# A hybrid decoder layer on one core: weight splitting of the up-projection and the g2 modulation moved to GpSimd

## The chip, the core and the metric

The kernel runs on one core of a Trainium2 chip. The metric is the device time of one execution in microseconds (us). TensorE multiplies matrices into PSUM banks; VectorE (DVE in the profile), ScalarE (ACT) and GpSimd (POOL) work elementwise, each in the strict order of its own instruction queue; SyncE (SP) issues the transfers from HBM.

## What is computed

One decoder layer on 256 tokens of 1024 channels in float32: an adaptive-norm mixer (recurrent and attention branches) and a gated channel sub-layer. The change lies in the second, and in the modulation vector `g2`, a product of `c` with a part of `w_ada`:

```python
mod = (c @ w_ada[l] + b_ada[l])[:, None, :]
sh1, sc1, g1, sh2, sc2, g2 = jnp.split(mod, N_MOD, axis=-1)
...
h2 = rmsnorm(x, norm2_g[l]) * (1.0 + sc2) + sh2
up = causal_dwconv(h2 @ w_up[l], ffn_conv_w[l], ffn_conv_b[l])
gate, val = jnp.split(up, 2, axis=-1)
x = x + g2 * ((jax.nn.silu(gate) * val) @ w_down[l])
```

## The kernel before

Weights come as a stream of 1 MB chunks [128, 2048] in the order of their use; six raw chunks (tile `w`) are held at a time, and a chunk's buffer is given to the next transfer by `used` and `send` when its last reader has been issued. TensorE multiplies in float32r, so every weight chunk and every activation is split into a high part (`wh`, a cast by ScalarE, `hi`) and a low part (`wl`, raw minus high by VectorE, `lo`); a product is three matmuls: high x high, high x low of the activation, low x high. A chunk is split in two halves of [128, 1024], `part` 0 and 1. Three chunks can be held split (`wspl`).

The channel sub-layer goes through 22 slices of 128 channels. From slice 4 on a plain loop sets the order, and every engine takes its instructions in the order in which the loop writes them. In turn `f`:

- TensorE multiplies `up(f)`: 8 row tiles `kt` of 6 matmuls, 48 in all. Tiles 0 to 3 need half 0 of chunk `up f`, tiles 4 to 7 half 1; within a tile the last two of the six matmuls need `wl`. At the end of the turn it multiplies `down(f - 2)`, 24 matmuls.
- ScalarE and VectorE meanwhile make slice `f - 1` ready: `gated_a` (ACT, from the PSUM bank), `gated_d` (DVE, the convolution), `gated_s` (ACT, Silu), `gated_m` (DVE), `gated_h` (ACT, high part `ph`), `gated_l` (DVE, low part `pl`). Between them they split the chunk of the next slice, `up f + 1`.
- In even turns they first split a chunk of the down-projection, `halves("dn", f // 2 - 1)`, which serves two slices.
- In turns 7, 9, 11 and 13 VectorE also takes a chunk of `g2`: `ada` multiplies each half [128, 1024] by `c` (tile `cb`, the same on all partitions) and sums along the row in the same instruction, and `ada_add` adds the bias. `g2` is used only by `out`, after the last slice.

`Bank.mm` issues all of these matmuls (L65), `affine` all casts of ScalarE (L138). In the profile L166 is `lo`, L367 `ada`, L377 `ada_add`, L732 `gated_a`, L740 `gated_d`, L744 `gated_s`, L748 `gated_m`, L756 `gated_l`.

Of the kernel before, what the change touches and what calls it, by code (L numbers as in the profile page):

```python
# [7 lines left out]
F32 = mybir.dt.float32  # L8
# [15 lines left out]
EPS = 1e-6  # L24
BIG = 1e30
SH1, SC1, G1, SH2, SC2, G2 = range(6)

# columns of the packed per-channel parameters
O_BADA = 0
# [15 lines left out]

# first guesses of an inverse root are these less half the bits, the sign being that before three Newton steps
GUESS = {1: float(0x5f3759df - 0x400000 - (1 << 31)), -1: float(0x5f3759df - 0x400000)}

NW = 6          # raw weight chunks in flight
NSPLIT = 3      # split weight chunks in flight  # L50


class Bank:
    """A PSUM bank that n matmuls accumulate into; the first one opens it, the last one closes it."""

# [13 lines left out]
def hybrid_layer(ctx: ExitStack, tc: tile.TileContext, x_d, c_d, pk_d, bd_d, ada1_d, lin_d, v_d,  # L69
# [20 lines left out]
    def tok(t):  # L90
        """[128, 4, 256] seen as [128, 2, 512]."""
        return flat(t).rearrange("p (t n) -> p t n", t=2)
# [6 lines left out]

# [1 line left out]
    order = []  # L101
# [15 lines left out]
    def send():  # L117
        """The next chunk's transfer."""
        if len(sent) < len(order):
            key = order[len(sent)]  # L120
            sent.append(key)
            raw[key] = wraw.tile([P, 2048], F32, tag="w", name="w")
            uses[key] = {"g1": 1, "ada1": 2, "s2": 2, "g2": 2}.get(key[0], 4)
            n = 1024 if key[0] in ("ada1", "lin") or key in (("g1", 0), ("g1", 1)) else 2048
            for c in range(0, 2048, n):
                nc.sync.dma_start(raw[key][:, c:c + n], srcs[key[0]][key[1]][:, c:c + n])

    def used(key):
        """A chunk's buffer goes to the next one after its last use."""
        uses[key] -= 1  # L130
        if uses[key] == 0:
            send()

    def affine(e, out, in_, scale=None, bias=None):
        """in_ * scale + bias by the activation engine, or by the vector engine where e is 1."""
        if e == 0:
            if scale is None and bias is None:
                nc.scalar.copy(out, in_)  # L138
            elif bias is None:
                nc.scalar.activation(out, in_, AF.Copy, scale=scale)  # L140
            else:
                nc.scalar.activation(out, in_, AF.Identity, scale=1.0 if scale is None else scale, bias=bias)  # L142
        elif scale is None and bias is None:
            nc.vector.tensor_copy(out, in_)
        elif scale is None:
            nc.vector.tensor_scalar(out, in_, bias, None, op0=ALU.add)
        elif bias is None:
            nc.vector.tensor_scalar(out, in_, scale, None, op0=ALU.mult)
        else:
            nc.vector.tensor_scalar(out, in_, scale, bias, op0=ALU.mult, op1=ALU.add)  # L150

    def hi(kind, i, part, e=0):
        """The high part of a half of the chunk, in float32r."""
        key = (kind, i)
# [5 lines left out]

    def lo(kind, i, part):
        """The low part: high + low is exact."""
        key = (kind, i)
        h, l = spl[key]
        c = slice(part * 1024, part * 1024 + 1024)
        nc.vector.tensor_sub(l[:, c], raw[key][:, c], h.bitcast(F32)[:, c])  # L166
        used(key)

# [1 line left out]
    xT = big.tile([P, KT, S], F32, name="xT")  # L170
# [39 lines left out]
    def table(func):  # L210
        """Has the activation engine load a function's table before the data is there."""
        nc.scalar.activation(warm, ones[:, 0:1], func)

    def warm_up(i):
        """Keeps the tensor engine's clock up while the first data comes."""
        b = get(B, "warm", lambda: bank(0, 1))
# [3 lines left out]

    B = {}   # PSUM banks by use
    T = {}   # tiles by use

    def consts():
        # (1 + b) g in b's place, where the gain is (1 + b + w c) g
        for n, j in ((0, SC1), (1, SC2)):
# [13 lines left out]

# [1 line left out]
    def newton(i, m, t, yi, sign):  # L242
        """A step of sign / sqrt(2 m): a first guess from the exponent, then three Newton steps of three."""
        y, v = yi.bitcast(F32), nc.vector
# [12 lines left out]
    def half_mean(ss, count):  # L257
        """-(ss / count + EPS) / 2"""
        m = small.tile([P, 2], F32, tag="hm", name="hm")
# [3 lines left out]
    def inverse(r, m):  # L263
        """1 / r after a Newton step, for r about the root of -2 m."""
        t = small.tile(list(r.shape), F32, tag=f"t{len(r.shape)}", name="t")
# [11 lines left out]
    def spread(d, bk, off):  # L277
        """Per-token values, on the diagonals of d, to all partitions: bank[:, off:off+256]."""
        bk.reopen(2)
# [3 lines left out]
    def token_sums(bk, off, sq):  # L283
        """bank[:, off + 2 th] += sum over the channels of sq [128, 256]."""
        for th in range(2):
# [6 lines left out]

# [1 line left out]
    cb = const.tile([P, D], F32, name="cb")  # L294
# [21 lines left out]
    def norm_s(n):  # L316
        """The roots of the means of the squares of the tokens, a column for each half of them."""
        T["rms"] = small.tile([P, 2], F32, tag="rms", name="rms")
# [12 lines left out]

# [1 line left out]
    lt = const.tile([P, 8, 4], F32, name="lt")  # L333
# [5 lines left out]
    def sp(i):  # L339
        """A step of z (1 + z^2 / 3 + ... + z^18 / 19) 2 + max(-lambda, 0), where z = e / (2 + e) and e = exp(-|lambda|)."""  # L340
        e, d, acc, v = lt[:, 1, :], lt[:, 2, :], lt[:, 3, :], nc.vector
# [18 lines left out]

# [1 line left out]
    def ada(kind, i, a):  # L362
        """Half a chunk: the modulation of 128 channels, by the vector engine; sc with its norm's gain."""
        v = raw[kind, i].rearrange("p (a n) -> p a n", a=2)
# [3 lines left out]
                                       op0=ALU.mult, op1=ALU.add, accum_out=mod[:, j, kt:kt + 1])  # L368
        used((kind, i))

    def ada_add(kind, i):
# [7 lines left out]
    def normed(n, kt):  # L379
        """x times its norm and gain; the shift comes with the split into high and low."""  # L380
        rep = B["n2"].t[:, 256:512] if n else rrep
# [17 lines left out]
    def lin(kt, out, i):  # L399
        """One of the three products of a k-tile for one of the four outputs."""  # L400
        wh, wl = spl["lin", kt]
# [11 lines left out]

# [1 line left out]
    def lru(name):  # L415
# [33 lines left out]
    def root():  # L449
        # sqrt(1 - a^2) = (1 + a) sqrt(tanh(-log(a) / 2))  # L450
        nc.scalar.activation(lru("r"), lru("r"), AF.Sqrt)  # L451
# [60 lines left out]

# [1 line left out]
    def kn():  # L514
# [8 lines left out]
    def q_sum():  # L523
        """The sums over the heads' channels, for two heads on the first rows of each quarter."""
        b = get(B, "qn", lambda: bank(3, 1))
# [31 lines left out]
    def qk_r(i):  # L557
        """The heads' norms, with the other sign."""
        if i < 2:
# [29 lines left out]

# [1 line left out]
    def g1_mm(i, b):  # L591
# [25 lines left out]

# [1 line left out]
    mn = small.tile([P, H, 2], F32, tag="mn", name="mn")  # L619
# [3 lines left out]
    def sc(i):  # L623
        """The scores of two heads, which lie on the two halves of the rows."""
        qs, kT = T["qs"], T["kT"]
# [37 lines left out]

# [1 line left out]
    def o_inv():  # L665
# [28 lines left out]

# [1 line left out]
    def wo(c, kt):  # L696
# [21 lines left out]

# [1 line left out]
    def up(f, kt):  # L720
# [708 lines left out]
    for f in range(4, NF):  # L1429
# [16 lines left out]
        if f + 1 < NF:  # L1446
            lo("up", f + 1, 1)
        if f in (7, 9, 11, 13):
            i = (f - 7) // 2
            ada("g2", i, 0)  # L1450
            ada("g2", i, 1)
            ada_add("g2", i)
        for m in range(KT):
# [24 lines left out]
def _lay_out(i):  # L1478
# [7 lines left out]
    def rows(w, per):  # L1486
        """[K, N] -> [chunks, 128, per * N]: `per` row tiles of 128 in a chunk."""
        k, n = w.shape
        return w.reshape(k // (per * P), per, P, n).transpose(0, 2, 1, 3).reshape(-1, P, per * n)

    def panels(w, n):
        """[1024, N] -> [N / n, 128, 8 * n]: all row tiles of n columns."""
        return w.reshape(KT, P, -1, n).transpose(2, 1, 0, 3).reshape(-1, P, KT * n)
# [52 lines left out]
```

## Time and profile before

| | |
|---|---|
| median of 3 runs | 333.09 us (330.11 to 334.47) |
| span of the profiled execution | 333.0 us |
| busy: TensorE, VectorE, ScalarE, GpSimd | 97%, 80%, 58%, 1% of the span |
| weights and inputs read from HBM | 75.91 MB |
| mean granted TensorE clock | 0.985 of full speed |

The profile gives no other time for the profiled execution than its span, from the first to the last instruction. The busy shares are means over stages with different limits; matmuls are pipelined, so a busy share of TensorE near 100% tells that it never stood still, not that it could not be fed faster.

### The profile page before, as it was taken

To read this page: it belongs to the slowest core of one execution; us is meant where nothing else is said; L and a number is where in the kernel's file an instruction comes from. 1 tells how busy PE (TensorE), PEld (TensorE's weight loads), DVE (VectorE), ACT (ScalarE), POOL (GpSimd) and SP (SyncE) were. 2 spreads that over 40 slices of the span, in tenths; PEclk is the share of its full clock that TensorE was granted. 3 is DMA by queue.
4 is the path that set the end of the run, shared out by engine and by line. 5 is a ranking of instruction groups with operands and counts; after the bars stand their busy time and mean duration, and the time that the engine had idled before them with its cause. 6 is when DMAs were issued, how large, how long until landed. Compare 5 with 4: busy or idle time off the path is not lost.

```text
span 333.0 us, 6442 instructions
## 1 busy us (share of the span) xinstructions
PE 324.4 (97%) x2594; PEld 305.6 (92%) x2594; DVE 266.5 (80%) x523; ACT 192.7 (58%) x329; POOL 2.8 (1%) x15
## 2 busy tenths in 40 slices
PE   7899999999989999999999999999999999999994
PEld 6599999977678999899999999999999999999994
DVE  0689999698999989899685888888888767685654
ACT  4752525499999436877455546464646464555530
POOL 3000000000000000000000000000000000000000
PEclk9769999999999999999999999999999999999999
DMA  6999999907648788972936457584849364300003
GB/s 200 404 407 408 405 336 426 366 5 275 238 160 347 299 323 299 367 280 86 365 134 238 143 204 293 177 330 153 355 139 365 129 226 154 128 0 3 0 2 126
DMA packets 14287, 77.37 MB, mean 232 GB/s; under 512 B 1585, under 2 KB 2225, under 8 KB 7218
## 3 DMA queue, kind: packets, MB, share of 16 engines
q1 hardware_dynamic: 14258, 76.97, 61.4%
q8 instruction: 20, 0.33, 0.4%
q14 instruction: 9, 0.07, 0.1%
HBM read 75.91 MB, written 1.05 MB: 231 GB/s over the span
## 4 chain that ended last, share of the span: by engine, by line
PE 85%; ACT 8%; DVE 3%; DMA 2%; issue 1%; SPq 0%
PE bank L65 85%; ACT p L644 2%; DMA xT<-in_dram 2%; ACT m L434 1%; DVE m L460 1%; ACT pt L138 1%; DVE m L768 1%; ACT wh L138 1%; ACT m L444 1%; ACT m L447 0%; DVE sq L309 0%; ACT L451 0%; ACT L444 0%; ACT L434 0%; DVE m L454 0%
## 5 line engine op out<-in xcount | busy, mean ns | idle before, releaser
L166 DVE TENSOR_TENSOR wl<-w,wh 128x1024 fp32r<-128x1024 f32 x94 | 113.3, 1221 | 19.6 <-ACT wh L138 18.8
L138 ACT CAST wh<-w 128x1024 fp32r<-128x1024 f32 x89 | 90.8, 1042 | 37.9 <-PE bank L65 34.2
L65 PE MATMUL bank<-hh__1580,wh 128*128 128x256 f32 x352 | 71.1, 284 | 0.0
L65 PE MATMUL bank<-hl__1581,wh 128*128 128x256 f32 x352 | 71.0, 283 | 0.0
L65 PE MATMUL bank<-hh__1580,wl 128*128 128x256 f32 x352 | 70.9, 283 | 0.0
L65 PEld LDWEIGHTS bank<-hh__1580,wh 128*128 128x128 f32 x352 | 54.9, 192 | 0.4 <-ACT hh__1580 L142 0.4
L65 PEld LDWEIGHTS bank<-hl__1581,wh 128*128 128x128 f32 x352 | 54.9, 192 | 0.2 <-DVE hl__1581 L394 0.2
L65 PEld LDWEIGHTS bank<-hh__1580,wl 128*128 128x128 f32 x352 | 54.9, 192 | 0.0
L740 DVE SCALAR_TENSOR_TENSOR m<-bank,pk,m 128x255 f32<-128x255 f32 x88 | 40.5, 480 | 17.3 <-ACT m L732 15.7
L65 PE MATMUL bank<-ph,wh 128*128 128x256 f32 x176 | 49.9, 284 | 0.0
L65 PE MATMUL bank<-pl,wh 128*128 128x256 f32 x176 | 49.8, 283 | 0.0
L65 PE MATMUL bank<-ph,wl 128*128 128x256 f32 x176 | 49.8, 283 | 0.0
L732 ACT ACTIVATE m<-bank,pk 128x256 f32<-128x256 f32 x44 | 22.4, 559 | 21.7 <-PE bank L65 21.7
L65 PEld LDWEIGHTS bank<-ph,wh 128*128 128x128 f32 x176 | 33.8, 192 | 0.1
L65 PEld LDWEIGHTS bank<-pl,wh 128*128 128x128 f32 x176 | 33.8, 192 | 0.0
L65 PEld LDWEIGHTS bank<-ph,wl 128*128 128x128 f32 x176 | 33.8, 192 | 0.0
L367 DVE CUSTOM_DVE_ANT_0 w<-w,cb 128x1024 f32<-128x1024 f32 x22 | 26.4, 1219 | 0.0
L744 ACT ACTIVATE m<-m 128x256 f32<-128x256 f32 x22 | 9.2, 418 | 24.9 <-DVE m L740 24.9
L65 PE MATMUL bank<-hh_mix__1172,wh 128*128 128x256 f32 x64 | 18.4, 288 | 0.0
L65 PE MATMUL bank<-hl_mix__1173,wh 128*128 128x256 f32 x64 | 18.2, 284 | 0.0
L65 PE MATMUL bank<-hh_mix__1172,wl 128*128 128x256 f32 x64 | 18.1, 283 | 0.0
L65 PE MATMUL bank<-hh__273,wh 128*128 128x256 f32 x96 | 14.7, 292 | 0.1
(174 smaller groups left out, 444.3 us busy)
## 6 DMA issues: line engine op xcount, KB each, us to landing
w<-in_dram SPq DMA_DIRECT2D x55, 1024.0 KB, 4.9
w<-in_dram SPq DMA_DIRECT2D x32, 512.0 KB, 8.6
xT<-in_dram SPq DMA_DIRECT2D x4, 256.0 KB, 4.8
out_dram<-m SPq DMA_DIRECT2D x4, 128.0 KB, 2.5
out_dram<-m SPq DMA_DIRECT2D x2, 256.0 KB, 2.5
m<-in_dram SPq DMA_DIRECT2D x1, 256.0 KB, 7.5
pk<-in_dram SPq DMA_DIRECT2D x1, 145.0 KB, 5.0
m<-in_dram SPq DMA_DIRECT2D x1, 4.0 KB
```

Source lines behind the costliest of these rows:

```text
L65: self.nc.tensor.matmul(out, lhsT, rhs, start=left == self.n, stop=left == 1, skip_group_check=True)
L138: nc.scalar.copy(out, in_)
L166: nc.vector.tensor_sub(l[:, c], raw[key][:, c], h.bitcast(F32)[:, c])
L367: nc.vector.tensor_tensor_reduce(v[:, a, :], v[:, a, :], cb, scale=scale, scalar=0.0, op0=ALU.mult, op1=ALU.add, accum_out=mod[:, j, kt:kt ...
L434: nc.scalar.activation(lru(("r", "ig")[m])[:, t, :], pair(B["gate", m, t // 2])[:, t % 2, :], AF.Sigmoid, bias=col((O_BA, O_BX)[m] + t))
L444: nc.scalar.activation(lru("a")[:, t, :], lru("r")[:, t, :], AF.Exp, scale=lt[:, 7, t:t + 1])
L460: nc.vector.tensor_tensor_scan(lru("xc")[:, t, :], lru("a")[:, t, :], lru("ig")[:, t, :], 0.0, op0=ALU.mult, op1=ALU.add)
L644: nc.scalar.activation(p[:, a:z], p[:, a:z], AF.Exp, scale=rqk[:, 0, th, h:h + 1], bias=eb[:, h, th:th + 1], accum_out=rs[:, th, h:h + 1])
L732: nc.scalar.activation(cv[:, s, :], pair(B["up", f])[:, s, :], AF.Identity, scale=col(O_FW + 88 + i), bias=col(O_FB + i))
L740: nc.vector.scalar_tensor_tensor(cv[:, s, d:], pair(B["up", f])[:, s, :S - d], col(O_FW + 44 * j + i), cv[:, s, d:], op0=ALU.mult, op1=ALU ...
L744: nc.scalar.activation(T["cv", f][:, 2, :], T["cv", f][:, 0, :], AF.Silu)
L768: nc.vector.scalar_tensor_tensor(ot[:, m % 2, :], pair(B["dn", i])[:, m % 2, :], mod[:, G2, m:m + 1], xT[:, m, :], op0=ALU.mult, op1=ALU.add)
```

## The change

From slice 4 on, half 1 of the low part of each next up-projection chunk is subtracted by GpSimd in place of VectorE: 17 instructions. The chunks of `g2` are multiplied by `c` by GpSimd (8 instructions on [128, 1024]) and summed along the row by ScalarE, as the accumulator output of a copy (8 instructions); the fused multiply-and-sum of VectorE goes (8 instructions with a read of the accumulator each). `ada_add` stays on VectorE and is written two turns later. Comments that the same edit drops are left out here; they move the line numbers of the functions behind them by up to nine.

```diff
-    def lo(kind, i, part):
-        """The low part: high + low is exact."""
+    def lo(kind, i, part, e=1):
+
         key = (kind, i)
         h, l = spl[key]
         c = slice(part * 1024, part * 1024 + 1024)
-        nc.vector.tensor_sub(l[:, c], raw[key][:, c], h.bitcast(F32)[:, c])
+        (nc.gpsimd if e == 2 else nc.vector).tensor_sub(l[:, c], raw[key][:, c], h.bitcast(F32)[:, c])
         used(key)
...
+    def ada_g2(i):
+
+        v = raw["g2", i].rearrange("p (a n) -> p a n", a=2)
+        for a in range(2):
+            nc.gpsimd.tensor_mul(v[:, a, :], v[:, a, :], cb)
+            kt = 2 * i + a
+            nc.scalar.activation(v[:, a, :], v[:, a, :], AF.Copy, accum_out=mod[:, G2, kt:kt + 1])
+            used(("g2", i))
...
         gated_l(f - 1)
         if f + 1 < NF:
-            lo("up", f + 1, 1)
+            lo("up", f + 1, 1, 2)
         if f in (7, 9, 11, 13):
-            i = (f - 7) // 2
-            ada("g2", i, 0)
-            ada("g2", i, 1)
-            ada_add("g2", i)
+            ada_g2((f - 7) // 2)
+        if f in (9, 11, 13, 15):
+            ada_add("g2", (f - 9) // 2)
```

On ScalarE, from the split of chunk `up 8` in turn 7 to that of `up 9` in turn 8, before the change (`wh_2306` is the high part of `up 8`, `wh_2399` that of down-projection chunk 3, `wh_2413` that of `up 9`, `m4_` the tile of a slice, `w_` the raw chunks):

```order
L138 CAST wh_2306<-w_2123 128x1024 [waits DMAHW7_49]
L138 CAST ph_2312<-m4_2300 128x256 [waits DVE_49,PE_49]
L138 CAST wh_2306<-w_2123 128x1024
L138 CAST wh_2399<-w_2008 128x1024 [waits DMAHW5_49,PE_49]
L138 CAST wh_2399<-w_2008 128x1024
L732 ACTIVATE m4_2407<-bank2_2251,pk_86 128x256 [waits PE_49]
L732 ACTIVATE m4_2407<-bank2_2251,pk_86 128x256
L744 ACTIVATE m4_2407<-m4_2407 128x256 [waits DVE_49,Activation_49]
L138 CAST wh_2413<-w_2204 128x1024 [waits DMAHW0_49,PE_49]
```

The same stretch of ScalarE after the change (`wh_2400` is down-projection chunk 3, `w_1840` the first chunk of `g2`):

```order
L138 CAST wh_2306<-w_2123 128x1024 [waits DMAHW7_49,Pool_49]
L138 CAST ph_2312<-m4_2300 128x256 [waits DVE_49,PE_49]
L138 CAST wh_2306<-w_2123 128x1024
L377 ACTIVATE w_1840,mod_129<-w_1840 128x1024 [waits DMAHW2_49,Pool_49]
L377 ACTIVATE w_1840,mod_129<-w_1840 128x1024 [waits Pool_49]
L138 CAST wh_2400<-w_2008 128x1024 [waits DMAHW5_49,PE_49]
L138 CAST wh_2400<-w_2008 128x1024
L741 ACTIVATE m4_2408<-bank2_2251,pk_86 128x256 [waits PE_49]
L741 ACTIVATE m4_2408<-bank2_2251,pk_86 128x256
L753 ACTIVATE m4_2408<-m4_2408 128x256 [waits DVE_49,Activation_49]
L138 CAST wh_2414<-w_2204 128x1024 [waits DMAHW0_49,PE_49]
```

Two activations that wait for GpSimd now stand between the cast of `up 8` and the casts of down-projection chunk 3.

On GpSimd, which had only constants to fill before, the instructions of turns 7 to 9 after the change:

```order
L166 TENSOR_TENSOR wl_2307<-w_2123,wh_2306 128x1024 [waits DVE_49,PE_49,DMAHW7_49,Activation_49,Pool_49]
L375 TENSOR_TENSOR w_1840<-w_1840,cb_131 128x1024 [waits DMAHW5_49,DMAHW2_49,DMAHW1_49]
L375 TENSOR_TENSOR w_1840<-w_1840,cb_131 128x1024
L166 TENSOR_TENSOR wl_2415<-w_2204,wh_2414 128x1024 [waits DVE_49,DMAHW0_49,PE_49,Activation_49]
L166 TENSOR_TENSOR wl_2509<-w_2325,wh_2508 128x1024 [waits DVE_49,PE_49,DMAHW3_49,Activation_49,Pool_49]
```

The two products of the `g2` chunk stand behind the subtraction of half 1 of `up 8` (`wl_2307`), which in turn waits for the cast of that half.

On VectorE, turn 7 to turn 8, before the change (`ISA` on L367 is the fused multiply-and-sum and its read of the accumulator):

```order
L166 TENSOR_TENSOR wl_2307<-w_2123,wh_2306 128x1024 [waits DMAHW7_49,PE_49,Activation_49]
L756 TENSOR_TENSOR pl_2316<-m4_2300,ph_2312 128x256 [waits Activation_49]
L166 TENSOR_TENSOR wl_2307<-w_2123,wh_2306 128x1024 [waits Activation_49]
L367 ISA w_1840,mod_129<-w_1840,cb_131 128x1024 [waits DMAHW2_49]
L367 ISA mod_129 128x1
...
L377 TENSOR_TENSOR mod_129<-mod_129,pk_86 128x2 [waits DVE_49]
L166 TENSOR_TENSOR wl_2400<-w_2008,wh_2399 128x1024 [waits DMAHW5_49,PE_49,Activation_49]
```

The same stretch of VectorE after the change, up to the convolution of slice 7:

```order
L166 TENSOR_TENSOR wl_2307<-w_2123,wh_2306 128x1024 [waits DMAHW7_49,PE_49,Activation_49]
L765 TENSOR_TENSOR pl_2316<-m4_2300,ph_2312 128x256 [waits Activation_49]
L166 TENSOR_TENSOR wl_2401<-w_2008,wh_2400 128x1024 [waits PE_49,DMAHW5_49,Activation_49,Pool_49]
L166 TENSOR_TENSOR wl_2401<-w_2008,wh_2400 128x1024 [waits Activation_49]
L749 SCALAR_TENSOR_TENSOR m4_2408<-bank2_2251,pk_86,m4_2408 128x255 [waits Activation_49]
L749 SCALAR_TENSOR_TENSOR m4_2408<-bank2_2251,pk_86,m4_2408 128x254 [waits DVE_49]
```

VectorE goes from `pl` of slice 6 straight to the low part of down-projection chunk 3, for which it waits on ScalarE's cast.

## Rows read from the trace of the kernel before

**Rows 1.** The page, parts 1 and 2: busy time by engine, slices.

```profile
PE 324.4 (97%) x2594; PEld 305.6 (92%) x2594; DVE 266.5 (80%) x523; ACT 192.7 (58%) x329; POOL 2.8 (1%) x15
...
PEclk9769999999999999999999999999999999999999
```

**Rows 2.** The chain that ended last: start us, us, what.

```profile
114.06 212.88 PE bank L65 x1800
326.97 2.07 DVE m L768 x5
```

**Rows 3.** Stretches, busy us (instructions) by engine, then granted clock, DMA share, GB/s.

```profile
80.00:90.00 10.00, 9.79 (x81) 6.44 (x79) 8.99 (x23) 9.43 (x19) 0.00 (x0) 1.00 0.80 315
90.00:104.00 14.00, 12.81 (x112) 10.23 (x108) 13.69 (x54) 14.00 (x39) 0.00 (x0) 1.00 0.53 180
...
197.28:214.56 17.28, 17.28 (x146) 17.28 (x145) 14.64 (x24) 9.36 (x14) 0.00 (x0) 1.00 0.65 244
```

**Rows 4.** ACT in time, turns 7 to 10: start us, us, instruction, idle before it.

```profile
194.06 1.05 ACT L138 CAST wh<-w 128x1024 fp32r<-128x1024 f32 x1
198.57 2.00 ACT L138 CAST wh<-w 128x1024 fp32r<-128x1024 f32 x2 [3.46 <-PE bank L65]
200.47 1.01 ACT L732 ACTIVATE m<-bank,pk 128x256 f32<-128x256 f32 x2
203.01 0.42 ACT L744 ACTIVATE m<-m 128x256 f32<-128x256 f32 x1 [1.53 <-DVE m L740]
203.33 1.03 ACT L138 CAST wh<-w 128x1024 fp32r<-128x1024 f32 x1
204.44 0.41 ACT L138 CAST ph<-m 128x256 fp32r<-128x256 f32 x1
204.75 1.04 ACT L138 CAST wh<-w 128x1024 fp32r<-128x1024 f32 x1
207.45 1.02 ACT L732 ACTIVATE m<-bank,pk 128x256 f32<-128x256 f32 x2 [1.65 <-PE bank L65]
209.60 0.42 ACT L744 ACTIVATE m<-m 128x256 f32<-128x256 f32 x1 [1.13 <-DVE m L740]
209.92 1.04 ACT L138 CAST wh<-w 128x1024 fp32r<-128x1024 f32 x1
...
211.34 1.04 ACT L138 CAST wh<-w 128x1024 fp32r<-128x1024 f32 x1
215.85 2.00 ACT L138 CAST wh<-w 128x1024 fp32r<-128x1024 f32 x2 [3.46 <-PE bank L65]
```

**Rows 5.** DVE in time, turns 7 and 8, columns as in Rows 4.

```profile
195.19 1.22 DVE L166 TENSOR_TENSOR wl<-w,wh 128x1024 fp32r<-128x1024 f32 x1
196.32 1.22 DVE L367 CUSTOM_DVE_ANT_0 w<-w,cb 128x1024 f32<-128x1024 f32 x1
...
199.65 2.36 DVE L166 TENSOR_TENSOR wl<-w,wh 128x1024 fp32r<-128x1024 f32 x2 [0.76 <-ACT wh L138]
...
204.40 1.23 DVE L166 TENSOR_TENSOR wl<-w,wh 128x1024 fp32r<-128x1024 f32 x1
```

**Rows 6.** PE in time, turn 7, columns as in Rows 4.

```profile
192.85 0.40 PE L65 MATMUL bank<-hh__1580,wh 128*128 128x256 f32 x2
...
198.61 0.28 PE L65 MATMUL bank<-ph,wh 128*128 128x256 f32 x1
...
198.73 0.28 PE L65 MATMUL bank<-pl,wh 128*128 128x256 f32 x1
```

**Rows 7.** POOL by line: busy us, mean ns, idle before.

```profile
L204 POOL MEMSET bd<- 128x1024 f32 x1 | 1.0, 956 | 0.1
L194 POOL MEMSET mask<- 128x256 f32 x1 | 0.3, 315 | 0.0
```

**Rows 8.** ACT by line and form, columns as in Rows 7.

```profile
L644 ACT ACTIVATION_READ_ACCUMULATOR p<-p,eb,iqk 128x1 f32 x16 | 3.1, 195 | 0.0
...
L451 ACT ACTIVATE m<-m 128x1024 f32<-128x1024 f32 x1 | 1.1, 1059 | 0.0
```

**Rows 9.** The page, part 6, DMA issues: count, KB each, us to landing.

```profile
w<-in_dram SPq DMA_DIRECT2D x55, 1024.0 KB, 4.9
```

## Prediction before the run

> **What bounds the kernel now.** I read the busy shares first, then the chain of waits, then the loop turn by turn. VectorE looks loaded, 80% of the span, and GpSimd empty at 1% [rows 1]: on the means alone, moving VectorE's work looks like a gain. The chain says otherwise. From 114.06 us on it is 212.88 us of TensorE without a break, and only 2.07 us of VectorE's last outputs follow [rows 2]. In two turns of the loop, 17.28 us, TensorE is busy 17.28 us at the full granted clock (1.00, that is 2.4 GHz), while VectorE works 14.64 us and ScalarE 9.36 us [rows 3]. So wherever the change acts, TensorE sets the time, VectorE already has spare time, and relieving it gives nothing back. Only new lateness of an operand can change the time. A matmul starts every 0.12 us (198.61 to 198.73), and up takes 48 of them, 192.85 to 198.61 [rows 6]; up and down together are 72, 8.64 us a turn, 17.28 us for two. ScalarE's rows repeat at that spacing (198.57 and 215.85) [rows 4].
>
> **What leaves VectorE.** 17 subtractions at about 1.22 us, 20.7 us of busy time, and 8 fused multiply-and-sums of 1.22 us, 9.8 us [rows 5]. Worth 0 us, for TensorE stands behind none of them. The cover is the turn itself: without TensorE's full turns they would be worth at most their own 30 us.
>
> **What GpSimd costs per instruction.** The trace has no arithmetic on GpSimd. Its nearest rows are fills: 0.956 us for 1024 elements, 0.315 us for 256 [rows 7], so 0.835 ns an element and 0.10 us beside. From below, an instruction that overlaps its two inputs and its output costs one such pass, 0.96 us. If its two reads pass one after the other it costs 0.10 + 2 x 0.855 = 1.81 us; if reads and write all do, 2.67 us. I take P = 2.3 us, just above the middle of the last two (2.24), since a fill has no input to fetch before it starts.
>
> The Trainium skill, GPSIMD Engine Reference, section "Elementwise — side-by-side cycle accounting", speaks against this change: it gives 4497 ns for a two-input add of 2048 float32 columns, about twice VectorE's time. Half of it, an estimate, is 2.25 us, and the sum below would be 8.7 us instead of 9.3. No run so far shows such an instruction.
>
> **The moved subtraction alone.** The cast of half 1 of up 9 ends at 204.75 + 1.04 = 205.79 [rows 4]; 0.05 us later a consumer can start (a cast that begins at 198.57 takes 1.04, the subtraction behind it starts at 199.65) [rows 4, 5]. GpSimd would be done at 208.1. TensorE needs this half for the fifth row tile's low part: up 9 begins at 192.85 + 17.28 = 210.13, four tiles of 6 matmuls and 4 matmuls more are 28 x 0.12 = 3.36, so 213.49 [rows 6]. That leaves 5.3 us: free, and it stays free up to P of 7.6 us.
>
> **The new wait on ScalarE.** This is the term that decides. In turns 7, 9, 11 and 13 ScalarE's two summing copies wait for GpSimd, and behind them in ScalarE's queue stand the two casts of the down chunk, gated_a, gated_s, the casts of the next up chunk and gated_h; VectorE waits for those, and TensorE for both. Before, ScalarE finished the cast of up 8 at 194.06 + 1.05 = 195.11 and then idled 3.46 us until 198.57, since that cast waited for TensorE [rows 4]; this idle time is the first cover. Now: 195.11 + 0.05, three GpSimd instructions in a row (the subtraction, two products) 3 x 2.3 = 6.9, to 202.06; 0.05 for the hand-over, and the second copy, 1.06 + 0.19 with the read of its sum [rows 8] (the first runs beside the second product). The cast of the down chunk starts at 203.36 instead of 198.57: **4.8 us late**.
>
> What TensorE tolerates: everything behind shifts with that cast. The down chunk's first low half is done at about 200.8 [rows 5], needed at the third matmul of down 6, 201.49 + 5.76 + 0.24 = 207.49: 6.6 us of slack. The tightest is half 0 of up 9: its low part is done at 204.40 + 1.23 = 205.63 [rows 5], and the fifth matmul of up 9 wants it at 210.13 + 0.48 = 210.61. Slack 4.98, less 0.05: **4.9 us**. So the first chunk of g2 costs nothing.
>
> But ScalarE does not catch up before the next one. From the down cast to the end of the cast of half 1 of up 9 it needs 205.79 - 198.57 = 7.22 us; the next turn, from gated_a to the end of the last cast, 212.38 - 207.45 = 4.93 us [rows 4], with only the 1.65 us wait for TensorE between them to be dropped (the waits for VectorE inside, 1.53 and 1.13, are hand-overs and stay). Then again 0.05 + 6.9 + 0.05 + 1.25. Sum 20.4 us, against 17.28: **3.1 us more lateness with each of the three further chunks**. At the fourth, 4.8 + 3 x 3.13 = 14.2 us; less the slack of 4.9, TensorE has stood still for **9.3 us**, in turns 10 to 15. After that ScalarE regains its slack, but a TensorE that is never idle gives nothing back. In P the sum is 12 P - 18.3, and zero below 1.53 us.
>
> **The remaining edits.** The buffer of a g2 chunk comes free with the second copy, some 5 us later, and the transfer of up 10 waits for it; it lands 4.9 us after issue [rows 9], at about 208.3, and its cast is at 209.92 before and some 4 us later now [rows 4]: covered; without that cover up to 3 us a chunk. The transfers queued behind it on SyncE belong to turns still later. ada_add two turns later is free: only the final outputs read it.
>
> **Rivals.** (1) GpSimd is quick. If it streams two inputs as it fills, P is near 1.81 and the sum 3.4 us, 336.4 us; below 1.53 us nothing is late and the time stays 333.0. Up to P = 2.08 the time is not slower by 2%. For it speaks the fill of 0.96 us; against it, that VectorE's subtraction, 1.22 us [rows 5], is itself well above one fill. (2) GpSimd and VectorE hold one another up. After the first g2 chunk GpSimd's subtraction in the even turns, from 7.27 to 9.57 us after the down cast, meets gated_d, which would start behind gated_a at 7.22 + 1.02 + 0.05 = 8.29 [rows 4]. If VectorE then waits for GpSimd's end, each of three passes is 1.3 us longer: 3.9 us more, 346.2 us. The trace of before has GpSimd silent in the loop, so no row speaks for or against.
>
> The Trainium skill, SBUF — State Buffer, section "Who interferes with whom", has such a rule: a VectorE instruction with two SBUF inputs and a GpSimd instruction that reads SBUF shut each other out, while one with a single SBUF input goes on. By that rule gated_d, which reads PSUM and one SBUF tile, is not held, and the rival falls; no run here shows it yet.
>
> (3) Faster: only if VectorE were on the chain inside the loop, where the chain is TensorE alone [rows 2]. I see no such place.
>
> **How the numbers follow.** The sum is made on the profiled span, 333.0 us, 0.1 below the median of the three runs: 333.0 + 9.3 = **342.3 us**, 2.8% slower. About 2% is what a measurement of this kernel tells from no change; that is 6.7 us, P = 2.08. Chances: the forecast with P from 2.08 to 2.67 alone, 0.58 (339.7 to 346.7 us); a quick GpSimd 0.24 (333.0 to 339.7); GpSimd and VectorE in each other's way, or P above 2.67, 0.16; faster 0.02. The range leaves out the lower half of the quick case and the far end of the slow one: 336 to 348 us. Slower by over 2%: 0.74, within 2%: 0.24, faster: 0.02.
>
> **What would show it.** In the changed profile GpSimd's two-input instructions should last about 2.3 us. ScalarE should wait for GpSimd about 4.6 us ahead of the first summing copy of a chunk, 2 x 2.3, and about 1 us ahead of the second. The casts of the down chunk should start about 4.8, 8, 11 and 14 us later than 198.57 and its repeats, with TensorE's own delay included. TensorE should be unbroken until the second g2 chunk and then wait for low halves or casts of up 11, 13 and 15, about 3 us in each pair of turns with some more spread over the down chunks. VectorE's busy time should fall by about 30 us and the granted clock stay at 1.00; earlier in the kernel, with TensorE busy 12.81 of 14 us, it was 1.00 too [rows 3]. I am wrong if GpSimd needs less than 1.5 us, if the copies do not stand in the way of the down casts, or if TensorE waits in turns without a g2 chunk, which would mean that the moved subtractions are late by themselves.

## The result and the profile after

The changed kernel takes 343.43 us (median of 4 runs, 343.14 to 344.04) against 333.78 us for the kernel before (4 runs, 330.11 to 334.64): a ratio of 1.032, 95% interval 1.025 to 1.039. The profiled execution took 343.67 us, of which the span is 341.9 us.

The page of the changed kernel, parts 1 and 5: busy time by engine, and groups with busy us, mean ns of one, then idle time before them and what ended it.

```profile
PE 326.2 (95%) x2594; PEld 304.1 (89%) x2594; DVE 238.7 (70%) x490; ACT 201.1 (59%) x345; POOL 62.6 (18%) x40
...
L166 DVE TENSOR_TENSOR wl<-w,wh 128x1024 fp32r<-128x1024 f32 x77 | 93.5, 1233 | 55.2 <-ACT wh L138 54.2
...
L166 POOL TENSOR_TENSOR wl<-w,wh 128x1024 fp32r<-128x1024 f32 x17 | 40.9, 2408 | 257.6 <-ACT wh L138 257.6
...
L377 ACT ACTIVATE w<-w 128x1024 f32<-128x1024 f32 x8 | 8.5, 1059 | 24.7 <-POOL w L375 24.7
L375 POOL TENSOR_TENSOR w<-w,cb 128x1024 f32<-128x1024 f32 x8 | 19.1, 2407 | 0.0
```

VectorE lost 28 us of work (266.5 to 238.7) and the kernel still became slower [rows 1]; what that relief is worth by itself, the run with the work left out shows below. The new row to look at is L377. Eight sums on ScalarE, 8.5 us of work, had 24.7 us of waiting for GpSimd in front of them. And VectorE, which has less to do, waits 54.2 us for ScalarE's casts (18.8 us in the kernel before).

The chain that ended last, from the start of TensorE's long piece on, with most of the second and all of the third detour left out (start us, us, what); before, it was one piece [rows 2]:

```profile
113.22 105.00 PE bank L65 x900
218.25 3.80 POOL w L375 x2
222.10 0.94 issue
223.23 0.95 ACT wh L138
224.25 2.36 DVE wl L166 x2
227.04 0.49 DVE m L749
227.94 1.04 ACT wh L138
229.00 1.24 DVE wl L166
230.28 8.44 PE bank L65 x68
238.75 3.80 POOL w L375 x2
...
271.28 64.58 PE bank L65 x536
335.89 2.08 DVE m L777 x5
```

TensorE runs unbroken through the first g2 chunk. From the second on, the chain leaves it once in each pass and goes products on GpSimd, sum on ScalarE (the "issue" piece), casts of the down chunk, its low part, the convolution, cast and low part of the next up chunk, and only then back to TensorE. From the start of TensorE's long piece to the last outputs it is 335.89 - 113.22 = 222.67 us, against 326.97 - 114.06 = 212.91 before [rows 2]: **9.76 us more**. This stretch is called the loop from here on; in truth it begins with matmuls of the mixer, some 50 us ahead of turn 4. Its length is compared below, since what lies ahead of it varies from run to run by some us (it began between 109.5 and 116.0 us in the profiles of this study) and the change does not touch that part.

ScalarE in time in the changed kernel, from the last cast of turn 7 on; it answers to [rows 4].

```profile
193.23 1.05 ACT L138 CAST wh<-w 128x1024 fp32r<-128x1024 f32 x1
199.20 1.06 ACT L377 ACTIVATE w<-w 128x1024 f32<-128x1024 f32 x1 [4.93 <-POOL w L375]
...
201.58 1.06 ACT L377 ACTIVATE w<-w 128x1024 f32<-128x1024 f32 x1 [1.23 <-POOL w L375]
...
202.64 1.98 ACT L138 CAST wh<-w 128x1024 fp32r<-128x1024 f32 x2
...
213.71 1.05 ACT L138 CAST wh<-w 128x1024 fp32r<-128x1024 f32 x1
219.71 1.06 ACT L377 ACTIVATE w<-w 128x1024 f32<-128x1024 f32 x1 [4.95 <-POOL w L375]
...
222.08 1.06 ACT L377 ACTIVATE w<-w 128x1024 f32<-128x1024 f32 x1 [1.22 <-POOL w L375]
...
223.13 1.98 ACT L138 CAST wh<-w 128x1024 fp32r<-128x1024 f32 x2
...
243.63 1.98 ACT L138 CAST wh<-w 128x1024 fp32r<-128x1024 f32 x2
...
264.13 1.98 ACT L138 CAST wh<-w 128x1024 fp32r<-128x1024 f32 x2
```

The two casts of the down chunk stand directly behind the sums. Before, they came every 17.28 us; now the spacing is 20.49, 20.50 and 20.50 us. Ahead of the two sums ScalarE waits 4.95 + 1.22 = 6.17 us; it used to idle 3.46 us at this place [rows 4], and that reserve is gone.

### The profile page after: what moved, and what is told of

Same layout as the page of the kernel before. It is cut to its first block, busy times and chain, and to the rows that moved or that the text cites. A ratio compares the mean times of both kernels' runs of the same rounds, so it can differ in the third digit from the quotient of the medians.

```text
span 341.9 us, 6507 instructions
## 1 busy us (share of the span) xinstructions
PE 326.2 (95%) x2594; PEld 304.1 (89%) x2594; DVE 238.7 (70%) x490; ACT 201.1 (59%) x345; POOL 62.6 (18%) x40
## 4 chain that ended last, share of the span: by engine, by line
PE 74%; ACT 9%; DVE 7%; POOL 3%; DMA 2%; issue 2%; SPq 1%; DVEq 0%; POOLq 0%; ACTq 0%
PE bank L65 74%; POOL w L375 3%; DVE wl L166 3%; ACT wh L138 2%; DMA w<-in_dram 2%; ACT p L653 2%; ACT m L443 1%; DVE m L749 1%; DVE m L469 1%; ACT pt L138 1%; DVE m L777 1%; ACT m L453 0%; ACT m L456 0%; SPq L173 0%; ACT L460 0%
## 5 line engine op out<-in xcount | busy, mean ns | idle before, releaser
L166 DVE TENSOR_TENSOR wl<-w,wh 128x1024 fp32r<-128x1024 f32 x77 | 93.5, 1233 | 55.2 <-ACT wh L138 54.2
L166 POOL TENSOR_TENSOR wl<-w,wh 128x1024 fp32r<-128x1024 f32 x17 | 40.9, 2408 | 257.6 <-ACT wh L138 257.6
L65 PE MATMUL bank<-hh__1580,wh 128*128 128x256 f32 x352 | 71.4, 284 | 1.8 <-ACT wh L138 1.8
L65 PE MATMUL bank<-hh__1580,wl 128*128 128x256 f32 x352 | 71.3, 284 | 1.6 <-DVE wl L166 1.6
L65 PE MATMUL bank<-hl__1581,wh 128*128 128x256 f32 x352 | 71.0, 283 | 0.0
L377 ACT ACTIVATE w<-w 128x1024 f32<-128x1024 f32 x8 | 8.5, 1059 | 24.7 <-POOL w L375 24.7
L375 POOL TENSOR_TENSOR w<-w,cb 128x1024 f32<-128x1024 f32 x8 | 19.1, 2407 | 0.0
L65 PE MATMUL bank<-hh_mix__1172,wh 128*128 128x256 f32 x64 | 18.4, 288 | 0.0
L65 PE MATMUL bank<-hl_mix__1173,wh 128*128 128x256 f32 x64 | 18.2, 284 | 0.0
```

The lines of the kernel that those rows point to most:

```text
L65: self.nc.tensor.matmul(out, lhsT, rhs, start=left == self.n, stop=left == 1, skip_group_check=True)
L166: (nc.gpsimd if e == 2 else nc.vector).tensor_sub(l[:, c], raw[key][:, c], h.bitcast(F32)[:, c])
L375: nc.gpsimd.tensor_mul(v[:, a, :], v[:, a, :], cb)
L377: nc.scalar.activation(v[:, a, :], v[:, a, :], AF.Copy, accum_out=mod[:, G2, kt:kt + 1])
```

## The experiments

The second column goes by the execution times, each run against runs of the kernel before taken beside it. The third goes by the profiled execution.

| run | time against before (95% interval) | loop, us | more than 212.91 |
|---|---|---|---|
| changed kernel | 1.032 (1.025 to 1.039) | 222.67 | 9.76 |
| subtraction alone | 1.001 (0.995 to 1.008) | 212.89 | 0.0 |
| g2 alone | 1.007 (1.003 to 1.011) | 212.90 | 0.0 |
| sums later | 0.999 (0.992 to 1.005) | 212.91 | 0.0 |
| products first | 0.996 (0.993 to 1.000) | 212.91 | 0.0 |
| chunks spaced out | 1.001 (0.996 to 1.006) | 213.38 | 0.47 |
| chunks in two pairs | 1.018 (1.011 to 1.024) | 219.51 | 6.60 |
| work left out | 0.994 (0.989 to 0.999) | 212.91 | 0.0 |
| subtraction shared | 1.019 (1.012 to 1.027) | 220.61 | 7.70 |
| half left out | 1.014 (1.010 to 1.019) | 218.20 | 5.29 |

In the five runs that lost nothing the loop came out within 0.02 us of 212.91, so it tells losses of a few tenths, which the times do not.

The theory was the prediction's: ScalarE is held in its queue by three GpSimd instructions in a row, the lateness adds up from chunk to chunk, and 4.9 us of it are free. The main rivals were that GpSimd's work costs by itself (late subtractions, or the two engines in each other's way) and that each chunk has a fixed cost.

**The subtraction alone**

```diff
-            ada_g2((f - 7) // 2)
-        if f in (9, 11, 13, 15):
-            ada_add("g2", (f - 9) // 2)
+            ada("g2", (f - 7) // 2, 0)
+            ada("g2", (f - 7) // 2, 1)
+            ada_add("g2", (f - 7) // 2)
```

> Only the moved subtractions; the g2 chunks stay fused on VectorE. Theory (the cost is ScalarE's wait for three GpSimd instructions in a row): 0 us against the kernel before, TensorE unbroken in the loop, the moved subtraction done some 5 us ahead of its use. Rival (the moved subtractions are late, or GpSimd and VectorE hold one another up): at least 3 us slower, with TensorE waiting for GpSimd or VectorE's rows longer than 1.22 us.

The loop takes 212.89 us, as before. GpSimd and VectorE did get in each other's way here: GpSimd's 17 subtractions took 2.64 us on average, not 2.41, and a multiply-and-sum of VectorE, 1.22 us in the kernel before [rows 5], took up to 3.42 beside one, for instance:

```profile
196.52 3.41 DVE L367 CUSTOM_DVE_ANT_0 w<-w,cb 128x1024 f32<-128x1024 f32 x1
```

So one sign of the rival, longer rows of VectorE, did appear, but its cost did not: TensorE waited for nothing in the loop. The moved subtraction is free by itself.

**g2 alone**

```diff
-            lo("up", f + 1, 1, 2)
+            lo("up", f + 1, 1)
```

> Only the g2 chunks moved; every subtraction stays on VectorE. Theory: GpSimd has nothing ahead of the products, makes them as soon as the chunk has landed, and ScalarE's sums find them ready; the sums' 2.1 us fit into the 3.5 us that ScalarE idles before the next down cast: 0 us against before. Rival (the g2 path alone costs): 5 us or more slower, ScalarE waiting for GpSimd ahead of each sum.

The loop takes 212.90 us and no sum waits for GpSimd: with nothing ahead of them the products of the third chunk, for one, were made from 201.66 on, turns before their sum. So each half of the change is free, and 9.76 us come from the two together. The interval of the time, 0.3 to 1.1% above before, is not in the loop; what it holds beyond the scatter ahead of the loop stays open.

**Sums later**: the same GpSimd instructions in the same order; `sum_g2` holds the two activations of `ada_g2`.

```diff
...
             ada_g2((f - 7) // 2)
+        if f in (8, 10, 12, 14):
+            sum_g2((f - 8) // 2)
```

> As the changed kernel, same work on GpSimd in the same order, but ScalarE's two sums of a chunk stand at the end of the following turn, so nothing in ScalarE's queue waits for the products. Theory: 0 us against before, though the transfer behind the g2 chunk starts some 5 us later. Rival (GpSimd's load itself, or the later release of the chunk's buffer, costs): as slow as the changed kernel, or at least 4 us slower than before.

No loss, with GpSimd as loaded as in the changed kernel and the chunk's buffer released still later. Moving two instructions in ScalarE's queue takes away the whole loss. GpSimd's products even took 3.27 us on average here, since VectorE now worked beside them.

**Products first**: GpSimd's two products go to the head of turns 7, 9, 11 and 13, the sums stay where they were.

```diff
...
+        if f in (7, 9, 11, 13):
+            ada_g2((f - 7) // 2)
         if f % 2 == 0:
             halves("dn", f // 2 - 1)
...
-            ada_g2((f - 7) // 2)
+            sum_g2((f - 7) // 2)
```

> As the changed kernel, but GpSimd's two products of a chunk stand at the head of the turn, ahead of the subtraction that waits for ScalarE's cast. Theory: they are done when ScalarE comes to the sums, only the sums' 2.1 us remain, inside the 3.5 us that ScalarE idles there: 0 us against before. If GpSimd's products shut VectorE's two-input subtractions out, VectorE's subtraction of half 0 in those turns lasts or starts up to 2.4 us later, still inside the slack. Rival (GpSimd's load costs by itself): 9 to 10 us slower.

No loss: 212.91 us. So it is not the sums' own 2.1 us either, but that the products stood behind a subtraction which waits for ScalarE's last cast. This and the one before are two ways to repair the change; both come out at the kernel before, neither ahead of it.

**Chunks spaced out**: g2 in turns 7, 11, 15 and 19.

```diff
-            if f in (5, 7, 9, 11):
+            if f in (5, 9, 13, 17):
...
-        if f in (7, 9, 11, 13):
...
+        if f in (7, 11, 15, 19):
...
```

> As the changed kernel, but the four g2 chunks are loaded and taken in turns 7, 11, 15 and 19, so that two turns without one lie between. Theory (lateness adds up, 4.9 us of slack, and ScalarE regains about 5 us in two free turns): the lateness of 4.9 us never passes the slack by more than a few tenths: 0 to 0.5 us against before. Rival (each chunk has its own cost, 9.7 us over four): 9 to 10 us slower, as the changed kernel.

The loop lost 0.47 us. The casts of the down chunks on ScalarE in this run, at the first three pairs of turns:

```profile
201.44 1.98 ACT L138 CAST wh<-w 128x1024 fp32r<-128x1024 f32 x2
213.98 2.00 ACT L138 CAST wh<-w 128x1024 fp32r<-128x1024 f32 x2 [0.42 <-issue]
236.10 1.98 ACT L138 CAST wh<-w 128x1024 fp32r<-128x1024 f32 x2
```

After a chunk the spacing is 12.54 us and not 17.28: ScalarE takes back 4.7 us in one free pair of turns and even idles 0.42 us. Over two pairs it is 34.66 us for 34.56 of TensorE's: each chunk is late by nearly the whole slack again, and 0.1 us more. The same four waits that cost 9.76 us in every second turn cost 0.47 us in every fourth. A fixed cost for each chunk is out.

**Chunks in two pairs**: g2 in turns 7, 9, 13 and 15.

```diff
-            if f in (5, 7, 9, 11):
+            if f in (5, 7, 11, 13):
...
-        if f in (7, 9, 11, 13):
...
+        if f in (7, 9, 13, 15):
...
```

> As the changed kernel, but the g2 chunks are taken in turns 7, 9, 13 and 15: two pairs with a pair of free turns between. Theory (lateness adds up within a pair, 4.9 + 3.2 - 4.9 = 3.2 us of stall in each, and ScalarE regains its slack between): 6.4 us slower than before. Rivals: a fixed cost for each chunk gives 9.7 us as in the changed kernel; a cost of ScalarE's wait alone without slack gives 4 x 4.9 = 19.6 us.

The loop lost 6.60 us where 6.4 was expected. Its chain, whole pieces of TensorE and what stands between (start us, us, what):

```profile
110.84 104.97 PE bank L65 x900
215.84 3.80 POOL w L375 x2
...
227.87 43.10 PE bank L65 x356
271.00 3.78 POOL w L375 x2
...
283.01 47.32 PE bank L65 x392
330.35 2.08 DVE m L777 x5
```

Two excursions through GpSimd, one at the second chunk of each pair; the first chunks do not appear.

**Work left out**: half 1's subtraction and the products of g2 are dropped and nobody makes them; TensorE reads half 0's low part a second time instead.

```diff
...
-            lo("up", f + 1, 1, 2)
+            used(("up", f + 1))
...
-            ada_g2((f - 7) // 2)
-        if f in (9, 11, 13, 15):
-            ada_add("g2", (f - 9) // 2)
+            i = (f - 7) // 2
+            used(("g2", i))
+            used(("g2", i))
+            nc.vector.tensor_copy(mod[:, G2, 2 * i:2 * i + 2], bada[:, G2, 2 * i:2 * i + 2])
```

> Bounds what a free helper engine could bring: from slice 5 on the subtraction of half 1 of the up chunks is left out (the matmuls read half 0's low part twice instead), and the products of g2 with c are left out too (g2 is the bias alone); all loads and matmuls stay. VectorE loses some 30 us of work and nobody gets it. Theory (TensorE sets the time of the loop): 0 us against before, within the noise. Rival (VectorE's load matters): faster by some of the 30 us.

```profile
112.16 212.88 PE bank L65 x1800
325.07 2.08 DVE m L778 x5
```

With the work gone altogether (VectorE is busy 237.8 us here), TensorE's piece in the chain is 212.88 us, to the hundredth that of [rows 2]. Relieving VectorE here was worth nothing before any cost was counted; the 0.1 to 1.1% by which the runs lie lower are not in the loop.

**Subtraction shared**: VectorE takes 512 columns of the moved subtraction, GpSimd the other 512.

```diff
...
+        for n, e in enumerate((nc.vector, nc.gpsimd)):
+            c = slice(part * 1024 + n * 512, part * 1024 + n * 512 + 512)
+            e.tensor_sub(l[:, c], raw[key][:, c], h.bitcast(F32)[:, c])
...
```

> As the changed kernel, but VectorE takes 512 of the 1024 columns of the moved subtraction and GpSimd the other 512, in every turn. Theory (three GpSimd instructions in a row ahead of ScalarE's second sum, each pass counted): the row is 1.2 us shorter, so first lateness 3.7 us, 2.0 us more with each further chunk, less 4.9 of slack: 4.8 us slower than before, half of the changed kernel's loss. Rival (the two products and the sums alone set the loss): 9 to 10 us slower.

Neither: 7.70 us, between 4.8 and 9.76. The row of three was only 0.6 us shorter, not 1.2, and four passes of that leave about 7.3. The rest is one pass that came out 0.36 us longer than its neighbours, behind a gated_m of VectorE that started late; why it did stays open. GpSimd's and VectorE's rows of turn 7 in this run:

```profile
190.69 1.78 POOL L175 TENSOR_TENSOR wl<-w,wh 128x512 fp32r<-128x512 f32 x1 [4.75 <-ACT wh L138]
```

```profile
190.64 0.69 DVE L175 TENSOR_TENSOR wl<-w,wh 128x512 fp32r<-128x512 f32 x1
```

Both start at once; GpSimd's is done 1.14 us after VectorE's has ended at 191.33. Either it was held until then, or a small instruction costs GpSimd nearly as much as a large one.

**Half left out**: as the run before without VectorE's 512 columns.

```diff
...
+        c = slice(part * 1024 + 512, part * 1024 + 1024)
+        nc.gpsimd.tensor_sub(l[:, c], raw[key][:, c], h.bitcast(F32)[:, c])
...
```

> As the changed kernel, but GpSimd subtracts only the last 512 of the 1024 columns and nobody the other 512 (row tiles 4 and 5 read the low parts of tiles 2 and 3 a second time instead); this leaves out part of the computation. In the run with the columns shared, GpSimd's 512 columns took 1.80 us and VectorE's 512 columns stood at the same time. Theory (0.6 us of that 1.80 was GpSimd held until VectorE's two-input subtraction ended): with VectorE's half gone GpSimd's instruction takes 1.2 us, the pass from down cast to down cast 19.3 us, and the loss is 4.8 us. Rival (a GpSimd instruction of this kind has a fixed cost of some 1.2 us and 1.2 ns a column): it takes 1.80 us again, and the loss is 7 to 8 us.

GpSimd by line in this run (busy us, mean ns, idle before), and three casts of the down chunk on ScalarE:

```profile
L174 POOL TENSOR_TENSOR wl<-w,wh 128x512 fp32r<-128x512 f32 x17 | 22.1, 1298 | 271.7 <-ACT wh L138 271.7
L382 POOL TENSOR_TENSOR w<-w,cb 128x1024 f32<-128x1024 f32 x8 | 19.1, 2406 | 0.0
```

```profile
221.72 1.98 ACT L138 CAST wh<-w 128x1024 fp32r<-128x1024 f32 x2
...
241.09 1.99 ACT L138 CAST wh<-w 128x1024 fp32r<-128x1024 f32 x2
...
260.48 1.99 ACT L138 CAST wh<-w 128x1024 fp32r<-128x1024 f32 x2
```

1.30 us for 512 columns, so 0.5 us of the 1.80 was holding. The pass is 19.38 us, 1.12 us shorter than in the changed kernel, which is the 1.11 us by which GpSimd's instruction is shorter (2.408 to 1.298), and the loss is 5.29 us. Four passes of 1.12 us less are 4.5 us less: 9.76 - 4.48 = 5.28. Between the two runs the loss follows GpSimd's duration one for one in every pass, as the sum had it. The 0.5 us above the 4.8 expected are mostly the 0.1 us by which the instruction is longer than the 1.2 assumed, four times.

## Why the prediction was right

- **What bounds the kernel.** TensorE alone in the loop: shown by the run with the work left out, 212.88 us of TensorE as before. With it falls the third rival, a faster kernel.
- **GpSimd's duration.** Taken as 2.3 us between 1.81 and 2.67; measured 2.41 us, start to start of consecutive ones about 2.36. The three of turn 7 took 196.76 + 4.78 - 194.41 = 7.13 us, not 6.9. That 2.41 lies so near is in part luck: the 2.3 was a choice between bounds from fills, by the forecast's own 12 P - 18.3 each 0.1 us of it is 1.2 us of time, and which of the instruction's passes overlap no run shows. GpSimd in time in the changed kernel:

```profile
194.41 2.40 POOL L166 TENSOR_TENSOR wl<-w,wh 128x1024 fp32r<-128x1024 f32 x1 [4.19 <-ACT wh L138]
196.76 4.78 POOL L375 TENSOR_TENSOR w<-w,cb 128x1024 f32<-128x1024 f32 x2
210.00 2.40 POOL L166 TENSOR_TENSOR wl<-w,wh 128x1024 fp32r<-128x1024 f32 x1 [8.45 <-ACT wh L138]
```

  The Trainium skill, GPSIMD Engine Reference, section "Elementwise — side-by-side cycle accounting": half of its 4497 ns for 2048 columns was 2.25 us, an estimate 7% below what this trace shows.
- **First lateness.** 4.8 us forecast. The loop began 0.84 us earlier in this run than in [rows 2], so the cast of [rows 4] would have come at 197.73; it came at 202.64: 4.9 us, and TensorE did not wait. The longer GpSimd instructions were partly made up by the second sum: the casts started 1.06 us after it (201.58 to 202.64), since the read of its accumulator lies beside the next cast's start; I had counted 1.25.
- **Growth with each chunk.** 3.13 us forecast, 20.50 - 17.28 = 3.22 measured.
- **Slack.** 4.9 us forecast. At the fourth chunk the cast came at 264.13 against 249.57 for the schedule before (250.41 in that trace, less 0.84): 14.56 us late, and 14.56 - 9.76 = 4.8 us were free. The run with spaced chunks, 0.47 us lost with four latenesses near 4.9, puts it at the same place.
- **Where TensorE waits.** At the low half and the cast of the down chunk and of the following up chunk, in every pair of turns from the second chunk on. TensorE's waits of the first such pass in the changed kernel, two at the down chunk and two at the up chunk:

```profile
224.22 0.39 PE L65 MATMUL bank<-ph,wh 128*128 128x256 f32 x1 [0.26 <-ACT wh L138]
...
225.53 0.39 PE L65 MATMUL bank<-ph,wl 128*128 128x256 f32 x1 [0.81 <-DVE wl L166]
...
229.02 0.50 PE L65 MATMUL bank<-hh__1580,wh 128*128 128x256 f32 x2 [0.61 <-ACT wh L138]
...
230.28 0.51 PE L65 MATMUL bank<-hh__1580,wl 128*128 128x256 f32 x2 [0.52 <-DVE wl L166]
```

  The places are those of the forecast, the split is not: it had about 3 us at the up chunk and some more at the down chunk, but the idle time is 1.07 us at the down chunk and 1.13 at the up chunk. At the second chunk the cast came 223.13 - (215.85 - 0.84) = 8.1 us late [rows 4], which is past the down chunk's slack of 6.6 us too. (A record of a matmul lasts 0.28 us while one starts every 0.12 us [rows 6], so these gaps, 2.20 us together, are shorter than the delay of 3.2 us that they stand for.) The granted clock stayed at 1.00 through it. The stretch of the third pass (busy us by engine, clock, DMA):

```profile
251.50:272.00 20.50, 18.31 (x147) 17.50 (x146) 9.99 (x17) 11.45 (x19) 9.57 (x5) 1.00 0.57 205
```

- **The sum.** 9.3 us forecast, 9.76 in the loop. That it came so close is luck in part: in each of the four passes GpSimd's row was 0.23 us longer than forecast and the second sum held the casts up 0.19 us less, and the two nearly cancel. The forecast time of 342.3 us set the profiled span equal to the execution's time; the run profiled after took 1.8 us more than its span (343.67 to 341.9). The span itself came 0.4 us below the forecast, as its loop was 0.5 us longer and what lies ahead of it 0.84 us shorter.
- **The rivals.** A quick GpSimd fell with 2.41 us. That GpSimd holds up gated_d fell too. VectorE in the changed kernel, while GpSimd's subtraction of turn 8 ran, from 210.00 to 212.40:

```profile
210.87 1.91 DVE L749 SCALAR_TENSOR_TENSOR m<-bank,pk,m 128x255 f32<-128x255 f32 x4 [0.80 <-ACT m L741]
```

Four instructions in 1.91 us, as in the kernel before.

## What to carry to other kernels

Before work is moved off a busy engine, look whether that engine is on the chain where it works: here some 28 us of relief were worth nothing. When an engine with an ordered queue takes over the end of a helper's work, its instruction belongs where the result is already there; put there, or with the helper's part issued ahead of what waits, the same split cost nothing, while in the wrong place it held every later instruction of the queue. Lateness below the slack is free only if the engine has time to regain it before the next one: the same four waits cost 0.47 us spaced out and 9.76 us in a row.

## What was not expected of the hardware

GpSimd and VectorE shut each other out when both read two tiles of SBUF: the one that came second did nearly all of its work after the other had ended. In the run with g2 alone, GpSimd's two products and VectorE's instructions beside them:

```profile
201.66 5.17 POOL L375 TENSOR_TENSOR w<-w,cb 128x1024 f32<-128x1024 f32 x2 [17.83 <-PE bank L65]
```

```profile
199.64 2.36 DVE L166 TENSOR_TENSOR wl<-w,wh 128x1024 fp32r<-128x1024 f32 x2 [3.24 <-ACT wh L138]
201.92 1.90 DVE L749 SCALAR_TENSOR_TENSOR m<-bank,pk,m 128x255 f32<-128x255 f32 x4
203.92 0.64 DVE L757 TENSOR_TENSOR m<-m 128x256 f32<-128x256 f32 x1
204.48 3.43 DVE L166 TENSOR_TENSOR wl<-w,wh 128x1024 fp32r<-128x1024 f32 x1
```

VectorE's subtraction of 1.22 us is recorded with 3.43 us from 204.48 on: it ended 1.08 us after GpSimd's second product (201.66 + 5.17 = 206.83), so it did nearly all of its work after it. The four instructions of gated_d, which read PSUM and one SBUF tile (and a column of `pk`), kept their 1.90 us under the first product. That is what the Trainium skill, SBUF — State Buffer, section "Who interferes with whom", states for VectorE instructions with two SBUF inputs and with one, and the trace agrees on both. In the changed kernel the two hardly met, because ScalarE kept VectorE waiting while GpSimd worked; in the repaired orders they do meet, up to 3.27 us for a mean product, and it fits into their spare time.

GpSimd's two-input instruction took 1.30 us for 512 columns and 2.41 us for 1024: on a straight line through the two, about 0.19 us and 2.17 ns a column.
